# Working out the first scale vector on the tensor engine, beside the first shift vector

## The chip, the cores and the metric

The kernel runs on one core of a Trainium2 chip. The metric is the device time of one execution, in microseconds (us), as the median of several runs. The engines are named as in the profile: PE is the tensor engine (PEld its weight loads), DVE the vector engine, ACT the scalar engine, POOL is GpSimd, and SP is the engine whose queue issues most of the transfers.

## The reference, cut to what matters

The reference is a two-layer trunk over 256 context tokens and 256 latent tokens of width 1024. Each layer is a half-step SwiGLU feed-forward network, a token mixer, and a second feed-forward network. Before each of them the tokens are normalised, scaled and shifted by vectors that come from the conditioning c (latent tokens) or c_ctx (context tokens). Only the very first scale and shift matter here:

```
c_silu  = silu(c);  cc_silu = silu(c_ctx)
m  = c_silu  @ w_ada[0] + b_ada[0]        # 9 vectors of 1024; 0 is the first shift, 1 the first scale
mc = cc_silu @ w_ada[0] + b_ada[0]
h  = rms_norm(x, g_sub[0,0]) * (1 + m[1]) + m[0]      # and the same with mc for the context
gu = h @ ffn_w_in[0,0]                                # 1024 -> 2 x 2816
```

So shift and scale are two products of a vector with a 1024 x 1024 part of w_ada, each for two vectors (context and latent). They need 4 MB of weights each, and nothing of the first feed-forward network can begin without their first 128 entries.

## The kernel before, in words

Activations are kept transposed: a tile has 128 of the 1024 features in its partitions and the 512 tokens (256 context, 256 latent) in its columns, so the 1024 features are 8 tiles, k = 0 to 7. A product in fp32 accuracy is made from two parts of each operand, hi and lo: mm3 (L300) issues three matmuls, w.hi x.hi (L301), w.hi x.lo (L302) and w.lo x.hi (L303). A weight tile comes by DMA as raw fp32 (wr) and is split by a cast on ACT (L165) and a subtraction on DVE (L166) into wp.

The start of the program is start (L1508). After the sums of squares of the tokens and their inverse roots (ss, rr), it works through k = 0 to 7. For each k:

- load(k) (L1512) issues four transfers of 256 KB on SP: two halves of the scale's tile, from the transposed matrix w_adaT (tile 8 + k), and two halves of the shift's tile, from w_ada0.
- The shift's tile k goes to the tensor engine. pe_a(k) (L1525) is the first half of ada_tile (L388): 8 matmuls whose stationary operand is csp, the silu of both conditioning vectors padded to 32 columns, and whose moving operand is 128 columns of the tile; four groups of 32 partitions of the result collect two of them each. The profile shows each of these fp32 matmuls twice. ACT copies the result (adx, L396). pe_b(k) (L1530) is the second half: one matmul with the constant sel (L399) sums the four groups and turns the result into a column, and ACT adds the bias (L400) into M[0, 0].
- The scale's tile k is dotted with both vectors, row by row. dot(k) (L1536): for the context vector DVE multiplies and sums in one instruction per half (junk, L1542); for the latent vector POOL multiplies in place (L1544) and dot_sum(k) on ACT (L1549) sums. dot_end(k) (L1551) puts halves, gain and bias together with two small DVE instructions (L1554, L1555) into M[0, 1].
- Norm.h (L490), called by h_a(k) and h_b(k): DVE makes hn = x * scale * rr (L498), ACT adds the shift and rounds to hh (L503), DVE makes the rest hl (L505). Each of the three is issued once for the 256 context and once for the 256 latent tokens.
- first_whole (L551) then multiplies h(k) with the first four weight tiles: 4 x mm3 = 12 matmuls of 512 columns (gu). These are called a step below; there are 8 steps.

The order is written out by hand (manual schedule), so each engine's queue follows the program text:

```
def before(k):  ...
    WS.step()        # one half weight tile split: ACT L165, DVE L166 (while any are left)
    h_a(k + 1); dot_sum(k + 2); dot(k + 3); h_b(k + 1); dot_end(k + 2); load(k + 4)
# 12 matmuls of step k
def after(k):
    pe_b(k + 2); pe_a(k + 3)
```

So on PE the order is step 0, pe_b(2), pe_a(3), step 1, pe_b(3), pe_a(4), and so on to pe_a(7) in front of step 5 and pe_b(7) in front of step 6. Tiles of the kind slot (among them ar, the halves of load) rotate over 44 buffers. After step 7 the feed-forward network goes on with the next pair of weight tiles; those are split (L165, L166) after the last h on ACT's and DVE's queues. Later scale, shift and gate vectors are dotted by DVE alone from w_adaT (ada_dot, L403), which the change does not touch; it keeps cb, the conditioning repeated over all partitions, in use.

Of the kernel before, what the change touches and what calls it, by code (L numbers as in the profile page):

```python
# [15 lines left out]
OP = mybir.AluOpType  # L16
# [78 lines left out]
def trunk(ctx, tc, io):  # L95
# [289 lines left out]
        nc.sync.dma_start(t, src)  # L385
        return t

    def ada_tile(q, t, m, raw):  # L388

        p = bank("ada")  # L390
        for k in range(KD):
            r = slice(32 * (k % 4), 32 * (k % 4) + 32)
            PE.matmul(p[r, 0:128], csp[:, k, :], raw[k // 4][:, k % 4 * 128:k % 4 * 128 + 128], start=(k < 4),
                      stop=(k >= 4), skip_group_check=True)
        x = small("adx", 128, 3)
        ACT.copy(x, p[:, 0:128])  # L396
        yield
        p = bank("ada")
        PE.matmul(p[:, 0:2], x, C["sel"], start=True, stop=True)  # L399
        ACT.activation(m[:, t], p[:, 0:2], AF.Identity, bias=C["b_ada"][:, q * 8 + t:q * 8 + t + 1])  # L400
        yield

    def ada_dot(t, m, raw, vs=V2):  # L403
# [1104 lines left out]
    def start(n0, first_part, norm, then):  # L1508
        M[0, 0], M[0, 1] = new_m(), new_m()
        raws = {}  # L1510

        def load(k):  # L1512
            if k < KD:
                raws[k] = [[slot("ar") for _ in range(2)] for _ in range(2)]
                for ts, src in zip(raws[k], (io["w_adaT"][0, 8 + k], io["w_ada0"][k])):
                    for a, t in enumerate(ts):
                        nc.sync.dma_start(t, src[:, a * 512:a * 512 + 512])

        g0, b0 = C["g_sub"][:, 0:8], C["b_ada"][:, 8:16]
        bg = small("bg", 8, 1)  # L1520
        DVE.scalar_tensor_tensor(bg, b0, 1.0, g0, OP.add, OP.mult)

        steps = {}

        def pe_a(k):  # L1525
            if k < KD:
                steps[k] = ada_tile(0, k, M[0, 0], raws[k][1])
                next(steps[k])

        def pe_b(k):  # L1530
            if k < KD:
                next(steps[k])

        acc = [M[0, 1], small("dacc", 16, 1).rearrange("p (k v) -> p k v", v=2)]

        def dot(k):  # L1536

            if k < KD:
                junk = adap.tile([128, 1024], BF16, name=nm("junk"), tag="junk", bufs=1)
                for a, raw in enumerate(raws[k][0]):  # L1540
                    cols = slice(a * 512, a * 512 + 512)
                    DVE.scalar_tensor_tensor(junk[:, cols], raw, 1.0, cb[:, 0, cols], OP.mult, OP.mult,  # L1542
                                             accum_out=acc[a][:, k, 0:1])
                    POOL.tensor_tensor(raw, raw, cb[:, 1, cols], OP.mult)  # L1544

        def dot_sum(k):
            if k < KD:
                for a, raw in enumerate(raws[k][0]):
                    ACT.activation(raw, raw, AF.Copy, accum_out=acc[a][:, k, 1:2])  # L1549

        def dot_end(k):  # L1551
            if k < KD:
                g = g0[:, k:k + 1]
                DVE.tensor_scalar(acc[1][:, k], acc[1][:, k], g, bg[:, k:k + 1], OP.mult, OP.add)  # L1554
                DVE.scalar_tensor_tensor(acc[0][:, k], acc[0][:, k], g, acc[1][:, k], OP.mult, OP.add)  # L1555

        load(0)
        rest = WS.load(4, True)
        load(1)
        load(2)  # L1560
        for raw, src in rest:
            nc.sync.dma_start(raw, src)
        load(3)
        for d in range(KD):
            for v in V2:
                n0.add(d, v)
        for v in V2:
            ACT.activation(cb[:, v], cb[:, v], AF.Silu)
        ss = [n0.ss(v) for v in V2]
        run(ss[0], 1)  # L1570
        run(ss[1], 1)
        pe_a(0)
        for _ in range(12):
            for g in ss:
                run(g, 1)
        for v in V2:
            n0.rr(v)
        pe_b(0)
        dot(0)
        WS.want(4, False)  # L1580
        WS.step(4)
        dot_sum(0)
        dot_end(0)
        dot(1)
        pe_a(1)
        hs = {}

        def h_a(k):
            if k < KD:
                hs[k] = [n0.h(k, v) for v in V2]  # L1590
                for g in hs[k]:
                    next(g)

        def h_b(k):
            if k < KD:
                for g in hs[k]:
                    next(g)

        def before(k):

            if k == 0:
                h_a(0)
                pe_b(1)
                h_b(0)
                pe_a(2)
                dot_sum(1)
                dot(2)
                dot_end(1)
            WS.step()
            h_a(k + 1)  # L1610
            dot_sum(k + 2)
            dot(k + 3)
            h_b(k + 1)
            dot_end(k + 2)
            load(k + 4)

        def after(k):
            pe_b(k + 2)
            pe_a(k + 3)

        n0.before, n0.after = before, after
        first_part.run(n0, norm, first_whole, then=then)

# [62 lines left out]
def layout(inp):  # L1686
    import numpy as np
    f = {k: np.asarray(v) for k, v in inp.items()}
    A = np.ascontiguousarray

    def col(v):
        v = v.reshape(v.shape[:-1] + (-1, 128))
        return np.moveaxis(v, -1, 0).reshape(128, -1)

    def rep(v):
        return np.broadcast_to(v.reshape(1, -1), (128, v.size))

    cc = np.stack([f["c_ctx"], f["c"][0]])
    parts = {
        "c": cc.reshape(2, 8, 128).transpose(2, 1, 0).reshape(128, 16),  # L1700
        "b_ada": col(f["b_ada"]), "g_sub": col(f["g_sub"]),
        "lru_cw": col(f["lru_conv_w"][0]), "lru_cb": col(f["lru_conv_b"][0]),
        "b_gate": col(f["lru_b_gate"][0]), "lam": col(f["lru_lambda"][0]),
        "dn_cw": col(f["dn_conv_w"][0]), "g_norm": col(f["dn_g_norm"][0]), "g_final": col(f["g_final"]),
        "a_log": rep(f["dn_a_log"][0]), "dt_bias": rep(f["dn_dt_bias"][0]),
        "sel": (np.arange(128)[:, None] % 32 == np.arange(2)[None, :]).astype(np.float32),
    }
    out = {"cst": A(np.concatenate([parts[k] for k in CST], axis=1)), "cb": A(cc)}
    tok = np.concatenate([f["ctx"][0], f["x"][0]], axis=0)
    out["x0"] = A(tok.reshape(2, 256, 4, 2, 128).transpose(0, 2, 4, 3, 1))  # L1710

    def pack(w, mt):
        K, Mm = w.shape
        return A(w.reshape(K // 128, 128, Mm // mt, mt).transpose(2, 1, 0, 3).reshape(Mm // mt, 128, -1))

    out["w_ada0"] = pack(f["w_ada"][0][:, :1024], 128)
    out["lru_in"] = pack(f["lru_w_in"][0], 128)
    out["lru_out"] = pack(f["lru_w_out"][0], 128)

    out["lru_gate"] = A(f["lru_w_gate"][0].reshape(2, 2, 4, 2, 128, 256).transpose(0, 2, 4, 1, 3, 5)  # L1720
                        .reshape(2, 4, 128, 1024))
    out["dn_in"] = pack(f["dn_w_in"][0][:, :4096], 128)
    out["dn_ab"] = pack(f["dn_w_in"][0][:, 4096:], 32)[0]
    out["dn_out"] = pack(f["dn_w_out"][0], 128)
    p = np.arange(128)
    same = (p[:, None] // 64) == (p[None, :] // 64)
    up = same & (p[:, None] <= p[None, :])
    low = same & (p[:, None] >= p[None, :])
    eye = np.eye(128, dtype=bool)
    flip = (p + 64) % 128  # L1730
    i = np.arange(64)
    m = {"U1": up, "L1": low, "U1s": up & ~eye, "L1s": low & ~eye, "U1f": up[:, flip], "L1f": low[:, flip],
         "CH0": p[:, None] < 64, "CH1": p[:, None] >= 64,
         "cap": np.concatenate([p[:, None] % 64 <= i[None, :], p[:, None] % 64 >= i[None, :]], axis=1)}
    m["blk"] = same
    m["eye"] = p[:, None] % 64 == i[None, :]
    m["sel32"] = p[:, None] % 32 == np.arange(32)[None, :]
    out["msk"] = A(np.concatenate([m[k].astype(np.float32) for k in MSK], axis=1))
    out["w_adaT"] = A(f["w_ada"].transpose(0, 2, 1).reshape(2, 72, 128, 1024))

    out["ffn_in"] = A(f["ffn_w_in"].reshape(2, 2, 8, 128, 2, NJ, 128).transpose(0, 1, 5, 4, 3, 2, 6)
                      .reshape(2, 2, NJ, 2, 128, 1024))
    wo = f["ffn_w_out"].reshape(2, 2, 2, HALF, 128, 8, 128).transpose(0, 1, 2, 5, 4, 3, 6)
    out["ffn_out0"] = A(wo[..., :8, :].reshape(2, 2, 2, 8, 128, 1024))
    out["ffn_out1"] = A(wo[..., 8:, :].reshape(2, 2, 2, 8, 128, 384))
    return out
# [22 lines left out]
```

## Time and profile before

| | us |
|---|---|
| median of 3 runs (lowest, highest) | 1840.24 (1838.59, 1842.27) |
| the profiled execution's own time | 1840.58 |
| its span in the profile | 1838.8 |
| start of step 0 on PE | 25.04 |
| start of the matmuls behind step 7 | 67.16 |

Durations come from the one profiled execution. A busy time adds up instructions; instructions of PE overlap, so the distance between two starts on PE is what a matmul costs there. "Idle before" is the time that an engine stood still ahead of an instruction, with what ended it. [...]

### The profile page before, as it was taken

Reading aid. Unit: us, or ns where it says so; the run is one execution under the profiler, and the core shown is the slowest. Engines: PE = TensorE matmul, PEld = TensorE weight load, DVE = VectorE, ACT = ScalarE, POOL = GpSimd, SP = SyncE. Lnnn points to the kernel's source line nnn. Section 1 sums busy time; section 2 is a strip of 40 time slices with the busy share of each in tenths; the row PEclk is TensorE's granted clock in tenths of the full one; section 3 lists DMA queues with packets and bytes.
Section 4 is the critical chain, followed back from the end, with each engine's and each line's share of the span. In section 5 each row is a group of like instructions: output and inputs, shape, how many; then the busy total and the mean of one; then the engine's idle time right before and its main releaser. Section 6 shows DMA issues by size and latency. Waiting matters only on the chain.

```text
span 1838.8 us, 28624 instructions
## 1 busy us (share of the span) xinstructions
PE 1767.9 (96%) x10806; PEld 1534.4 (83%) x10806; DVE 1311.3 (71%) x2694; ACT 807.0 (44%) x1661; POOL 105.6 (6%) x146
## 2 busy tenths in 40 slices
PE   4999999999899999999999999999999989889997
PEld 3788888888778888888898888888997988689997
DVE  7877866787878767766657655555689978776565
ACT  5532222246884433233334331332478434655454
POOL 4100000000000000000000000000006330100000
PEclk9999999999999999999999999999999989989999
DMA  9354645452133666466633675654335550025653
GB/s 348 113 185 158 220 160 171 160 200 89 46 115 126 215 214 223 178 228 207 215 113 126 218 247 198 218 199 136 105 99 166 171 175 1 1 104 188 202 184 116
DMA packets 98059, 300.59 MB, mean 163 GB/s; under 512 B 10881, under 2 KB 20353, under 8 KB 97793
## 3 DMA queue, kind: packets, MB, share of 16 engines
q1 hardware_dynamic: 92160, 277.79, 44.7%
q0 software_dynamic: 5760, 20.97, 3.7%
q8 instruction: 85, 1.39, 0.3%
q14 instruction: 54, 0.43, 0.1%
HBM read 276.70 MB, written 22.02 MB: 162 GB/s over the span
## 4 chain that ended last, share of the span: by engine, by line
PE 79%; DVE 10%; ACT 5%; issue 4%; DMA 2%; POOL 0%; SPq 0%; POOLq 0%; ACTq 0%; DVEq 0%
PE gu L302 14%; PE gu L301 14%; PE gu L303 14%; PE fo L303 4%; PE fo L302 4%; PE fo L301 4%; PE tl L301 4%; PE tl L302 4%; PE tl L303 4%; DVE u L791 2%; PE p L1386 1%; PE gu L546 1%; PE gu L542 1%; PE gu L543 1%; PE p L1417 1%
## 5 line engine op out<-in xcount | busy, mean ns | idle before, releaser
L165 ACT CAST wp<-wr 128x512 fp32r<-128x512 f32 (+1 forms) x689 | 382.7, 607 | 279.8 <-DMA wr<-in_ffn_out_dram 68.1
L166 DVE TENSOR_TENSOR wp<-wr,wp 128x512 fp32r<-128x512 f32 (+1 forms) x689 | 433.5, 676 | 98.9 <-ACT wp L165 95.3
L302 PE MATMUL gu<-hl,wp 128*128 128x512 f32 (+1 forms) x1312 | 477.0, 364 | 8.0 <-DVE hl L505 8.0
L301 PE MATMUL gu<-hh,wp 128*128 128x512 f32 (+1 forms) x1312 | 476.9, 363 | 0.9 <-ACT hh L503 0.8
L303 PE MATMUL gu<-hh,wp 128*128 128x512 f32 (+1 forms) x1312 | 476.2, 363 | 0.0
L407 DVE SCALAR_TENSOR_TENSOR junk<-ar,cb 128x1024 bf16<-128x1024 f32 x224 | 273.8, 1223 | 22.6 <-DMA ar<-in_w_adaT_dram 18.8
L302 PEld LDWEIGHTS gu<-hl,wp 128*128 128x128 f32 x1312 | 247.3, 189 | 49.0 <-DVE hl L505 10.3
L301 PEld LDWEIGHTS gu<-hh,wp 128*128 128x128 f32 x1312 | 247.4, 189 | 41.2 <-ACT hh L503 1.6
L303 PEld LDWEIGHTS gu<-hh,wp 128*128 128x128 f32 x1312 | 247.5, 189 | 38.8
L657 ACT ACTIVATE sg<-gu 128x512 f32<-128x512 f32 (+1 forms) x88 | 47.9, 544 | 362.0 <-PE gu L303 352.3
L659 DVE TENSOR_TENSOR hf<-sg,gu 128x512 f32<-128x512 f32 (+1 forms) x88 | 54.5, 620 | 177.2 <-PE gu L303 130.3
L301 PE MATMUL tl<-hidh,wp 128*128 128x256 f32 (+1 forms) x418 | 139.1, 333 | 0.0
L302 PE MATMUL tl<-hidl,wp 128*128 128x256 f32 (+1 forms) x418 | 138.6, 332 | 0.0
L303 PE MATMUL tl<-hidh,wp 128*128 128x256 f32 (+1 forms) x418 | 138.6, 332 | 0.0
L301 PE MATMUL fo<-hidh,wp 128*128 128x512 f32 (+1 forms) x352 | 127.0, 361 | 0.0
L303 PE MATMUL fo<-hidh,wp 128*128 128x512 f32 (+1 forms) x352 | 127.0, 361 | 0.0
L302 PE MATMUL fo<-hidl,wp 128*128 128x512 f32 (+1 forms) x352 | 127.0, 361 | 0.0
L301 PE MATMUL f<-H,wp 128*128 128x256 f32 x320 | 93.2, 291 | 0.0
L303 PE MATMUL f<-H,wp 128*128 128x256 f32 x320 | 91.4, 286 | 1.0 <-DVE wp L166 1.0
L302 PE MATMUL f<-H,wp 128*128 128x256 f32 x320 | 91.2, 285 | 0.0
L301 PEld LDWEIGHTS tl<-hidh,wp 128*128 128x128 f32 x418 | 79.0, 189 | 7.9
L302 PEld LDWEIGHTS tl<-hidl,wp 128*128 128x128 f32 x418 | 79.0, 189 | 7.8
(322 smaller groups left out, 2794.7 us busy)
## 6 DMA issues: line engine op xcount, KB each, us to landing
wr<-in_ffn_in_dram SPq DMA_DIRECT2D x172, 512.0 KB, 4.7
ar<-in_w_adaT_dram SPq DMA_DIRECT2D x128, 512.0 KB, 3.6
wr<-in_ffn_out_dram SPq DMA_DIRECT2D x64, 512.0 KB, 4.9
kp<-wp SPq DMA_DIRECT2D x80, 256.0 KB, 7.2
wp<-kp POOLq DMA_DIRECT2D x40, 512.0 KB, 5.0
wr<-in_dn_in_dram SPq DMA_DIRECT2D x32, 512.0 KB, 3.7
wr<-in_ffn_out_dram SPq DMA_DIRECT2D x64, 192.0 KB, 3.5
wr<-in_lru_in_dram SPq DMA_DIRECT2D x16, 512.0 KB, 3.9
```

Of the source, the lines that this page charges most:

```text
L165: ACT.copy(dst.hi, src)
L166: DVE.tensor_tensor(dst.lo, src, dst.hi.bitcast(F32), OP.subtract)
L301: PE.matmul(out, w.hi, x.hi, start=start, stop=False)
L302: PE.matmul(out, w.hi, x.lo, start=False, stop=False)
L303: PE.matmul(out, w.lo, x.hi, start=False, stop=stop)
L407: DVE.scalar_tensor_tensor(junk, raw, 1.0, cb[:, v], OP.mult, OP.mult, accum_out=m[:, t % 8, v:v + 1])
L542: PE.matmul(p[:, cols], w.hi, x.hi, start=(k == 0), stop=False)
L543: PE.matmul(p[:, cols], w.lo, x.hi, start=False, stop=False)
L546: PE.matmul(p[:, cols], w(k * 128).hi, x.lo, start=False, stop=(k == KD - 1))
L657: ACT.activation(sg[:, cols], P[0][:, cols], AF.Silu)
L659: DVE.tensor_tensor(hf[:, cols], sg[:, cols], P[1][:, cols], OP.mult)
L791: DVE.scalar_tensor_tensor(uv[:, :, a:b], pv[:, :, a + sh:b + sh], cw(j), uv[:, :, a:b], OP.mult, OP.add)
```

## The change

The shift's and the scale's vector are now both made by ada_tiles, for one k at a time. load(k) fetches tiles k and 8 + k of w_ada0, which now holds 2048 columns, in place of a tile of w_adaT and one of w_ada0: the same four transfers of 256 KB. pe_a(k) issues 16 matmuls in place of 8, the scale's 8 into columns 128 to 255 of the same bank, and ACT copies 256 columns in place of 128. pe_b(k) issues two matmuls with sel in place of one, and ACT two activations: the shift with its bias, and the scale with the gain as factor and (1 + bias) * gain as bias. dot, dot_sum and dot_end, and with them all work of POOL and the multiplications of DVE in the steps, are gone. The order of what is left is as it was.

```diff
--- before.py
+++ after.py
@@ -385,19 +385,24 @@
         nc.sync.dma_start(t, src)
         return t
 
-    def ada_tile(q, t, m, raw):
+    def ada_tiles(raws, outs):
+
 
         p = bank("ada")
-        for k in range(KD):
-            r = slice(32 * (k % 4), 32 * (k % 4) + 32)
-            PE.matmul(p[r, 0:128], csp[:, k, :], raw[k // 4][:, k % 4 * 128:k % 4 * 128 + 128], start=(k < 4),
-                      stop=(k >= 4), skip_group_check=True)
-        x = small("adx", 128, 3)
-        ACT.copy(x, p[:, 0:128])
+        n = len(raws)
+        for i, raw in enumerate(raws):
+            for k in range(KD):
+                r = slice(32 * (k % 4), 32 * (k % 4) + 32)
+                PE.matmul(p[r, i * 128:i * 128 + 128], csp[:, k, :], raw[k // 4][:, k % 4 * 128:k % 4 * 128 + 128],
+                          start=(k < 4), stop=(k >= 4), skip_group_check=True)
+        x = small("adx", 128 * n, 3)
+        ACT.copy(x, p[:, 0:128 * n])
         yield
         p = bank("ada")
-        PE.matmul(p[:, 0:2], x, C["sel"], start=True, stop=True)
-        ACT.activation(m[:, t], p[:, 0:2], AF.Identity, bias=C["b_ada"][:, q * 8 + t:q * 8 + t + 1])
+        for i, (out, scale, bias) in enumerate(outs):
+            PE.matmul(p[:, 2 * i:2 * i + 2], x[:, i * 128:i * 128 + 128], C["sel"], start=True, stop=True)
+        for i, (out, scale, bias) in enumerate(outs):
+            ACT.activation(out, p[:, 2 * i:2 * i + 2], AF.Identity, scale=scale, bias=bias)
         yield
 
     def ada_dot(t, m, raw, vs=V2):
@@ -1512,47 +1517,26 @@
         def load(k):
             if k < KD:
                 raws[k] = [[slot("ar") for _ in range(2)] for _ in range(2)]
-                for ts, src in zip(raws[k], (io["w_adaT"][0, 8 + k], io["w_ada0"][k])):
+                for ts, src in zip(raws[k], (io["w_ada0"][k], io["w_ada0"][8 + k])):
                     for a, t in enumerate(ts):
                         nc.sync.dma_start(t, src[:, a * 512:a * 512 + 512])
 
-        g0, b0 = C["g_sub"][:, 0:8], C["b_ada"][:, 8:16]
+        g0, b0, b1 = C["g_sub"][:, 0:8], C["b_ada"][:, 0:8], C["b_ada"][:, 8:16]
         bg = small("bg", 8, 1)
-        DVE.scalar_tensor_tensor(bg, b0, 1.0, g0, OP.add, OP.mult)
+        DVE.scalar_tensor_tensor(bg, b1, 1.0, g0, OP.add, OP.mult)
 
         steps = {}
 
         def pe_a(k):
             if k < KD:
-                steps[k] = ada_tile(0, k, M[0, 0], raws[k][1])
+
+                steps[k] = ada_tiles(raws[k], ((M[0, 0][:, k], 1.0, b0[:, k:k + 1]),
+                                               (M[0, 1][:, k], g0[:, k:k + 1], bg[:, k:k + 1])))
                 next(steps[k])
 
         def pe_b(k):
             if k < KD:
                 next(steps[k])
-
-        acc = [M[0, 1], small("dacc", 16, 1).rearrange("p (k v) -> p k v", v=2)]
-
-        def dot(k):
-
-            if k < KD:
-                junk = adap.tile([128, 1024], BF16, name=nm("junk"), tag="junk", bufs=1)
-                for a, raw in enumerate(raws[k][0]):
-                    cols = slice(a * 512, a * 512 + 512)
-                    DVE.scalar_tensor_tensor(junk[:, cols], raw, 1.0, cb[:, 0, cols], OP.mult, OP.mult,
-                                             accum_out=acc[a][:, k, 0:1])
-                    POOL.tensor_tensor(raw, raw, cb[:, 1, cols], OP.mult)
-
-        def dot_sum(k):
-            if k < KD:
-                for a, raw in enumerate(raws[k][0]):
-                    ACT.activation(raw, raw, AF.Copy, accum_out=acc[a][:, k, 1:2])
-
-        def dot_end(k):
-            if k < KD:
-                g = g0[:, k:k + 1]
-                DVE.tensor_scalar(acc[1][:, k], acc[1][:, k], g, bg[:, k:k + 1], OP.mult, OP.add)
-                DVE.scalar_tensor_tensor(acc[0][:, k], acc[0][:, k], g, acc[1][:, k], OP.mult, OP.add)
 
         load(0)
         rest = WS.load(4, True)
@@ -1576,12 +1560,8 @@
         for v in V2:
             n0.rr(v)
         pe_b(0)
-        dot(0)
         WS.want(4, False)
         WS.step(4)
-        dot_sum(0)
-        dot_end(0)
-        dot(1)
         pe_a(1)
         hs = {}
 
@@ -1603,15 +1583,9 @@
                 pe_b(1)
                 h_b(0)
                 pe_a(2)
-                dot_sum(1)
-                dot(2)
-                dot_end(1)
             WS.step()
             h_a(k + 1)
-            dot_sum(k + 2)
-            dot(k + 3)
             h_b(k + 1)
-            dot_end(k + 2)
             load(k + 4)
 
         def after(k):
@@ -1713,7 +1687,7 @@
         K, Mm = w.shape
         return A(w.reshape(K // 128, 128, Mm // mt, mt).transpose(2, 1, 0, 3).reshape(Mm // mt, 128, -1))
 
-    out["w_ada0"] = pack(f["w_ada"][0][:, :1024], 128)
+    out["w_ada0"] = pack(f["w_ada"][0][:, :2048], 128)
     out["lru_in"] = pack(f["lru_w_in"][0], 128)
     out["lru_out"] = pack(f["lru_w_out"][0], 128)
```

## Rows read from the trace of the kernel before

**Rows 1.** The page, part 1: busy time of each engine over the span

```profile
PE 1767.9 (96%) x10806; PEld 1534.4 (83%) x10806; DVE 1311.3 (71%) x2694; ACT 807.0 (44%) x1661; POOL 105.6 (6%) x146
```

**Rows 2.** Windows, a stretch each: length, busy us (instructions) by engine, PEclk, DMA share, GB/s

```profile
0.00:67.16 67.16, 40.77 (x252) 29.86 (x253) 55.74 (x134) 36.67 (x97) 25.78 (x24) 0.95 0.67 246
...
200.00:400.00 200.00, 200.00 (x925) 167.41 (x924) 150.49 (x266) 59.68 (x115) 0.00 (x0) 1.00 0.53 179
```

**Rows 3.** Chain that ended last, 25.04 to 67.16: shares by line, then pieces (start, us)

```profile
by line: DVE hl L505 31.3%; DVE junk L1542 14.5%; PE gu L302 11.4%; PE gu L303 10.2%; PE gu L301 9.9%; DVE hn L498 7.6%; DVE wp L166 5.4%; issue 4.6%; DVE dacc L1554 4.3%; PE ada L393 1.4%; PE ada L399 0.6%; DVE m L1555 0.3%
...
36.60 0.78 DVE hn L498 x2
37.38 1.23 DVE junk L1542 x4
38.61 2.83 DVE hl L505 x2
41.81 0.69 DVE wp L166
...
56.47 0.43 PE gu L303
...
57.16 0.23 PE gu L302
```

**Rows 4.** Waits of PE, 25.04 to 67.16: total us, times, longest

```profile
PE gu L302 <- DVE hl L505: 8.0, 5, 2.9
```

**Rows 5.** Timeline, DVE's hl beside POOL at work, and with POOL idle

```profile
43.97 3.07 POOL L1544 TENSOR_TENSOR ar<-ar,cb 128x512 f32<-128x512 f32 x2 [2.81 <-DVE junk L1542]
...
44.42 2.90 DVE L505 SCALAR_TENSOR_TENSOR hl<-hn,m,hh 128x256 fp32r<-128x256 f32 x2
...
60.27 0.88 DVE L505 SCALAR_TENSOR_TENSOR hl<-hn,m,hh 128x256 fp32r<-128x256 f32 x2 [0.24 <-ACT hh L503]
```

**Rows 6.** Windows, steps 3, 4 and 7 of eight adjoining ones, and the sum of eight

```profile
44.88:50.83 5.95, 3.96 (x35) 2.93 (x31) 5.92 (x12) 3.02 (x11) 3.13 (x3) 1.00 0.29 94
50.83:58.25 7.42, 5.50 (x35) 4.07 (x31) 7.35 (x12) 2.87 (x11) 5.03 (x4) 0.77 0.05 17
...
64.30:67.16 2.86, 2.86 (x13) 2.17 (x12) 2.80 (x7) 2.84 (x5) 0.00 (x0) 1.00 0.00 0
sum 42.12, PE 33.37 PEld 25.06 DVE 40.42 ACT 22.67 POOL 19.39; mean PE 4.17 PEld 3.13 DVE 5.05 ACT 2.83 POOL 2.42
```

**Rows 7.** Timeline of PE and PEld: first rise of the clock, pe_b, pe_a, later stalls

```profile
29.31 0.51 PE L302 MATMUL gu<-hl,wp 128*128 128x512 f32 x1
...
43.87 0.42 PEld L399 LDWEIGHTS ada<-cst,adx 128*128 128x128 f32 x2
...
44.31 0.38 PEld L393 LDWEIGHTS ada<-ar,csp 128*32 128x32 f32 x16
...
44.88 0.19 PEld L301 LDWEIGHTS gu<-hh,wp 128*128 128x128 f32 x1 [0.20 <-issue]
...
47.38 0.50 PE L302 MATMUL gu<-hl,wp 128*128 128x512 f32 x1 [1.99 <-DVE hl L505]
...
53.25 0.66 PE L302 MATMUL gu<-hl,wp 128*128 128x512 f32 x1 [1.92 <-DVE hl L505]
```

**Rows 8.** Transfers of ar: SP's issues of the shift's tiles 3 and 7; time to landing

```profile
23.61 0.95 SPq L1517 DMA_DIRECT2D ar<-in_w_ada_dram  x2
...
34.34 0.96 SPq L1517 DMA_DIRECT2D ar<-in_w_ada_dram  x2
...
DMA to landing us min/median/max: 4.9/5.2/7.2
```

**Rows 9.** ACT's bias activation (min/median/max ns), and the weight splits behind step 7

```profile
L400 ACT ACTIVATE m<-ada,cst x8: 238/243/263, 17.5 to 61.8; 128x2 f32<-128x2 f32 x8
...
63.87 2.17 ACT L165 CAST wp<-wr 128x512 fp32r<-128x512 f32 x4
...
64.50 2.50 DVE L166 TENSOR_TENSOR wp<-wr,wp 128x512 fp32r<-128x512 f32 x4
```

## Prediction

> **What bounds the kernel now.** I read the page's busy times first: PE is busy for 96% of the span and no other engine comes near it [rows 1]. A change that takes work from DVE, ACT and POOL and gives some to PE can therefore only pay where PE stands still. The windows say where that is: in the first 67.16 us PE is busy for 40.77 us, while DVE is busy for 55.74; from 200 to 400 us PE is busy in every microsecond [rows 2]. The change lies inside that first stretch.
>
> Next comes the chain that ended last, cut to the eight steps (25.04 to 67.16 us). The reader should see that DVE, not PE, carries it: hl alone has 31.3% of it, junk (the scale's dots) 14.5% [rows 3]. The pieces of one step follow each other without a hole: two hn, 0.78 us, two junk with their sums, 1.23, two hl, 2.83, a wait and one weight split, 0.69; then the next hn 5.9 us after the last. Steps 1 to 4 all have this pattern. PE's waits agree: 8.0 us in five waits for hl [rows 4]. The reason for the long hl is in the timeline: two of them take 2.90 us while POOL works on its two multiplications (3.07 us), and 0.88 us once POOL is idle [rows 5]. So the scale's dots cost DVE twice, once by their own time and once by what POOL's share does to hl.
>
> The windows of the steps give the yardstick. All eight take 42.12 us, of which PE is busy for 33.37; steps 3 and 4 take 5.95 and 7.42 us, and step 7, in which PE waits for nothing, 2.86 [rows 6].
>
> **The change, part by part.**
>
> Removed per k: two junk with sums on DVE, the two small DVE instructions, two POOL multiplications and two ACT sums. What DVE keeps in a step is a split, two hn and two hl, 0.69 + 0.87 + 0.88 = 2.4 us with POOL idle [rows 3, 5], where a step now lasts 5.9. DVE then has time to spare, and the next thing to be late is PE itself.
>
> Added on PE: one more pe_a and one more pe_b for each k. In the step that runs at the full clock, the loads of pe_b begin at 43.87 (in the shadow of the last matmul, which ends its turn at 44.10), those of pe_a at 44.31, and the next step's load at 44.88 after 0.20 of idleness [rows 7]. So pe_b costs 0.21 and pe_a 0.57, of which 0.38 is its 16 loads and 0.20 the gap behind them. For the doubled pe_b I take 0.40 (bounds 0.21 and 0.42). For the doubled pe_a I take 0.57 + 0.38 = 0.95, the gap being paid once; the bounds are 0.57 and 1.14.
>
> The gap is a row's; why it is there, the row does not say ("issue"). [...]
>
> The stretch after the change, from the start of step 0 on:
> - Its start stays at 25.04. It stands behind pe_a(2), whose last quarter waits for the last half of load(2), and these transfers keep size, order and number. What the doubled pe_a(0) and pe_b(0) add on PE before that lies in waits for data. I cost it at nothing; if that cover were missing it would be one pe_a, 0.6.
> - Step 0 runs at the lower clock at first: matmuls stand 0.43 us apart there and 0.23 later [rows 3], and the first rise came at 29.3 [rows 7]. Without the wait for hl in it, ten matmuls at 0.43 and two at 0.23 make 4.86 us (bounds 2.86 and 12 x 0.43 = 5.16).
> - Seven steps without waits: 7 x 2.86 = 20.02.
> - pe_b(2) to pe_b(7): 6 x 0.40 = 2.40. pe_a(3) to pe_a(7): 5 x 0.95 = 4.75.
>
> The sum is 32.03 us against 42.12, so step 7 ends at 57.07 instead of 67.16: **10.1 us less**.
>
> Edits that I cost at nothing, and what covers them. ACT loses two sums per k and gains one activation of 0.24 us [rows 9] and 128 more columns to copy; a step of 4.2 us holds its cast, two hh, two activations and the copy (about 2.4). The chain from pe_a(k+2) to h(k+1) is copy, cast, split, hn, hh, hl: about 0.5 + 0.62 + 0.69 + 0.87 + 0.45 + 0.45 = 3.6 us with hn and hh overlapped by halves [rows 3, 5, 9], and hl is wanted 2.86 + 0.40 + 0.95 + 0.2 = 4.4 us after pe_a(k+2); if the cover fails, each step grows by the difference. SP's queue keeps its order. The tiles of w_ada0 have the size of those of w_adaT, and their buffers come free at pe_a(k), no later than before. The data arrive in time: the later pair of load(3) is issued from 23.61 to 24.56 and lands 5.2 us after that, at 29.8, while pe_a(3) ends at 31.2; that of load(7), issued by 35.3, lands at 40.5 [rows 8], when PE gets to pe_a(7) at 47. The weights behind step 7 are split in 2.17 and 2.50 us behind the last h [rows 9]; pe_b(7) ends two steps before the end, at 51.4, h(7) is done some 2.5 us later, and the first split stands at 55, ahead of 57.07.
>
> Behind step 7 PE is the bound [rows 2] and nothing is tied to a fixed time, so I let the whole gain reach the end. The profiled execution took 1840.58 us: 1840.58 - 10.1 = 1830.5. It stands 0.3 above the median, 1840.24, so the forecast is 1830.4.
>
> **The rivals.**
>
> *A new chain through ACT and DVE ends last* (chance 0.12). The 3.6 us above leave out the hand-overs between engines; with 0.2 for each of six it is 4.8, and if the two hl stay 0.6 us slower than with POOL idle, for another reason than POOL, it is 5.4. That is 1.0 more than the 4.4 at hand, in each of the four steps in which weights are split: 4 us of the gain go, and the time is 1834.4. For it: the chain is emitted across two iterations, behind the copy on ACT. Against: hl at 0.88 with POOL idle is in the trace, and one step of slack is written into the order.
>
> *The gain is hidden* (0.07): step 7 ends earlier but something behind it does not, the next weight tiles or their transfers. That gives 1840. Against: the weights' transfers wait for buffers that the splits free, and these splits move forward too; the DMA share in step 4 is 0.05 [rows 6], so there is room.
>
> *The clock stays low: slower than before* (0.05). [...] For it: in step 4 the granted clock is a mean of 0.77 [rows 6], after a wait that ended at 53.25 [rows 7]. Against: the wait of 1.99 us that ended at 47.38 [rows 7] left the clock at 1.00 throughout step 3 [rows 6], and in the sum above no such wait is left. [...]
>
> **How the numbers follow.** The forecast has 0.76. About 0.2%, 3.7 us, is what a measurement of this kernel can tell from no change. The forecast and the first rival lie beyond that: faster 0.88. Same is 0.07, slower 0.05. For the range, the bounds of the costs reach down to 10.1 + 2.0 (step 0) + 1.1 (pe_b) + 1.9 (pe_a) = 15.1 us of gain if all come together; I go to 13.4, 1827.0. Upward, 1.0 for pe_a, 0.6 for the start, 0.3 for step 0 and one fall of the clock (8 matmuls x 0.2 = 1.6) make 1834.0; half of the first rival's cases lie within another 1.5, so 1835.5.
>
> **What would show it right or wrong.** Right: hl at about 0.44 us each, no wait of PE for hl, steps of 2.86 with 1.3 to 1.4 us of pe_b and pe_a between them, POOL idle after the first 5 us, step 7 ending near 57, and the same distance from there to the end as before. Wrong: waits of PE for hh or hl that remain, waits for ar in pe_a(3) and later, matmuls 0.43 us apart beyond step 0, pe_a of more than 1.2 us, or a later wait that takes the gain back.

## The result, and the profile after

The changed kernel takes 1830.11 us, the median of 12 runs (1827.26 to 1839.76); the kernel before, timed beside it, 1841.41 (12 runs, 1838.59 to 1847.65). The ratio is 0.9942, with a 95% interval of 0.9927 to 0.9958: faster by 0.6%, 11 us. The prediction was 1830.4, with a range of 1827.0 to 1835.5.

The page's busy times, after; they answer to [rows 1]. POOL has lost 24.5 us and DVE 26, PE has gained 3:

```profile
span 1828.4 us, 28807 instructions
...
PE 1770.9 (97%) x10950; PEld 1538.7 (84%) x10950; DVE 1285.2 (70%) x2646; ACT 800.9 (44%) x1637; POOL 81.1 (4%) x130
```

The windows of the eight steps, after (length, busy us with instructions of PE, PEld, DVE, ACT, POOL, then PEclk, the mean granted clock as a share of full speed, then DMA share, GB/s); they answer to [rows 2, 6]:

```profile
24.38:29.67 5.29, 5.16 (x52) 4.01 (x48) 2.36 (x5) 2.31 (x6) 0.00 (x0) 1.00 1.05 402
29.67:33.97 4.30, 4.30 (x52) 3.59 (x48) 2.36 (x5) 2.31 (x6) 0.00 (x0) 1.00 1.05 405
...
38.29:42.61 4.32, 4.32 (x52) 3.59 (x48) 2.72 (x6) 2.31 (x6) 0.00 (x0) 1.00 1.03 420
42.61:46.93 4.32, 4.32 (x52) 3.59 (x48) 1.76 (x5) 1.69 (x5) 0.00 (x0) 1.00 0.37 148
46.93:50.17 3.24, 3.24 (x20) 2.72 (x17) 1.40 (x4) 1.18 (x3) 0.00 (x0) 1.00 0.03 5
50.17:53.02 2.85, 2.85 (x14) 2.34 (x14) 1.92 (x5) 2.12 (x6) 0.00 (x0) 1.00 0.00 0
53.02:55.74 2.72, 2.72 (x13) 2.25 (x12) 2.59 (x6) 2.69 (x5) 0.00 (x0) 1.00 0.02 3
```

Read the first and the second column against each other. PE is busy for the whole of every step but step 0, and steps 1 to 4, which have a pe_b and a pe_a behind them, last the same 4.3 us (step 0 has both too, but its matmuls start out further apart, 0.43 us). DVE, which was busy for nearly all of steps 3 and 4 before [rows 6], works 2.7 and 1.8 us of those. Step 7 ends at 55.74 us; before it was 67.16. So the front of the program is 11.42 us shorter, and the two spans differ by 1838.8 - 1828.4 = 10.4: what lies behind step 7 took 1771.6 us before and 1772.7 after, and the gain reached the end but for one microsecond. That microsecond can't be told from scatter: in the ten profiles of this case, all versions taken together, what lies behind step 7 took 1769.1 to 1778.2 us.

The chain that ended last, cut to the same stretch, has no line of DVE any more (compare [rows 3]):

```profile
by line: PE gu L301 24.1%; PE gu L303 20.7%; PE gu L302 20.3%; DMA ar<-in_w_ada_dram 20.1%; PE ada L396 14.3%; PE ada L403 5.4%; issue 0.1%
```

The DMA part is one piece of 6.29 us that begins ahead of the stretch, at 22.98: the last of the rows that pe_a(3) takes. They arrive at 29.27, when pe_a(3) is under way. The view of PE's waits, which had 8.0 us for hl [rows 4], has no row between 24.38 and 55.74; what is left of waiting stands with PE's weight loads, 0.40 us for these rows in pe_a(3), and then the gap behind every pe_a:

```profile
29.31 0.16 PEld L396 LDWEIGHTS ada<-ar,csp 128*32 128x32 f32 x8 [0.40 <-DMA ar<-in_w_ada_dram]
29.67 0.19 PEld L301 LDWEIGHTS gu<-hh,wp 128*128 128x128 f32 x1 [0.20 <-issue]
```

Why DVE is gone from the chain, its timeline shows: hl, in the changed kernel on L510, and in front of it split (L166) and hn (L503), in step 1; it answers to [rows 5]:

```profile
30.73 0.69 DVE L166 TENSOR_TENSOR wp<-wr,wp 128x512 fp32r<-128x512 f32 x1 [2.69 <-ACT wp L165]
31.34 0.87 DVE L503 SCALAR_TENSOR_TENSOR hn<-x,m,rr 128x256 f32<-128x256 f32 x2
...
32.45 0.88 DVE L510 SCALAR_TENSOR_TENSOR hl<-hn,m,hh 128x256 fp32r<-128x256 f32 x2 [0.24 <-ACT hh L508]
```

And PE between steps 1 and 2, with the doubled pe_b (L403) and pe_a (L396); it answers to [rows 7]:

```profile
32.53 0.50 PE L403 MATMUL ada<-cst,adx 128*128 128x2 f32 x4
32.96 1.08 PE L396 MATMUL ada<-ar,csp 128*32 128x128 f32 x32
33.97 0.50 PE L301 MATMUL gu<-hh,wp 128*128 128x512 f32 x1
```

From start to start pe_b takes 0.43 us and pe_a 1.01, of which 0.81 are its 32 loads and 0.20 the gap behind them. Before, the two took 0.21 and 0.57.

### The profile page after: what moved, and what is told of

Read it like the earlier page. It is cut to its first block, busy times and chain, and to the rows that moved or that the text cites. A ratio compares the mean times of both kernels' runs of the same rounds, so it can differ in the third digit from the quotient of the medians.

```text
span 1828.4 us, 28807 instructions
## 1 busy us (share of the span) xinstructions
PE 1770.9 (97%) x10950; PEld 1538.7 (84%) x10950; DVE 1285.2 (70%) x2646; ACT 800.9 (44%) x1637; POOL 81.1 (4%) x130
## 4 chain that ended last, share of the span: by engine, by line
PE 81%; DVE 8%; ACT 5%; issue 3%; DMA 2%; SPq 0%; POOL 0%; POOLq 0%; ACTq 0%; DVEq 0%
PE gu L301 14%; PE gu L302 14%; PE gu L303 14%; PE fo L303 4%; PE fo L302 4%; PE fo L301 4%; PE tl L301 4%; PE tl L303 4%; PE tl L302 4%; DVE u L796 1%; DMA wr<-in_ffn_in_dram 1%; PE p L1391 1%; PE gu L551 1%; PE gu L547 1%; PE gu L548 1%
## 5 line engine op out<-in xcount | busy, mean ns | idle before, releaser
L166 DVE TENSOR_TENSOR wp<-wr,wp 128x512 fp32r<-128x512 f32 (+1 forms) x689 | 432.5, 674 | 110.7 <-ACT wp L165 106.8
```

The source lines that it names most:

```text
L166: DVE.tensor_tensor(dst.lo, src, dst.hi.bitcast(F32), OP.subtract)
```

## The experiments

Two accounts fit what has been said so far. By the first, the step was set by DVE, and DVE was slow both because of its own dots and because POOL's multiplications made hl three times as long (2.90 us for two, 0.88 with POOL idle [rows 5]). By the second, DVE's own dots are enough. What the tensor engine's part costs, and what bounds the front now, are further questions. In each run below, "the steps" are the distance from the start of step 0 to the end of step 7: 42.12 us before, 31.36 after. The profiled executions differ in where step 0 starts, so this distance is what is compared. It scatters too: it was 31.36 and 31.83 in two profiles of the changed kernel. Three of the versions were run once, and the twelve runs of the changed kernel lie between 1827.26 and 1839.76 us; of a single run the distance tells more than the time.

**POOL's multiplications left out of the kernel before.**

```diff
-                    POOL.tensor_tensor(raw, raw, cb[:, 1, cols], OP.mult)
```

> Kernel before without POOL's multiplications (the latent half of the scale is then a sum of the raw rows); junk, sums and small instructions stay. Theory 1 (POOL at work makes hl three times as long, and that with junk set the step): hl falls from 1.45 to 0.44 us, the eleven slow ones give back about 11 us, step 7 ends near 56.5 in place of 67.16, and the time is near 1830, almost all of what the change brought. Rival A (the dots' own time on DVE set the step, hl is long for another reason): hl stays at 1.45, step 7 ends at 67, the time at 1840. Rival B (the gain came from falls of the tensor clock that are gone): something between, only if the waits of PE stay above 1 us and the 0.43 us spacing stays.

The steps took 30.37 us (23.76 to 54.13), the time was 1828.05 us (4 runs), the ratio to the kernel before 0.9928 (0.9907 to 0.9948). All sixteen hl are short, though every junk, sum and small instruction is still there. First the group of hl (durations min/median/max in ns), then steps 1 and 2 and all eight steps in the windows:

```profile
L505 DVE SCALAR_TENSOR_TENSOR hl<-hn,m,hh x16: 478/482/486, 23.3 to 50.9; 128x256 fp32r<-128x256 f32 x16
```

```profile
29.32:32.96 3.64, 3.64 (x34) 2.93 (x30) 3.13 (x11) 2.29 (x7) 0.00 (x0) 1.00 1.05 401
32.96:37.24 4.28, 3.92 (x34) 2.92 (x30) 4.02 (x14) 3.07 (x11) 0.00 (x0) 1.00 1.06 406
...
23.76:54.13 30.37, 29.49 (x188) 23.01 (x189) 27.77 (x78) 22.61 (x64) 0.00 (x0) 1.00 0.70 272
```

So the first account holds, and more sharply than I had it: taking POOL out of the way is enough for the whole gain. The dots that stay on DVE nearly fit beside PE; in step 2 PE still waits 0.36 us for hl, with DVE busy for 4.02 of 4.28 us. The long waits are gone: PE waited 0.9 us for hl in all.

Two things limit what this run shows. It does not do the latent half of the dots at all, so it gives the price of that half on POOL, and not what the work costs elsewhere. And a part of the gain is the tensor clock's, a share of what rival B says: before, the granted clock was a mean of 0.77 in step 4, which lasted 1.5 us longer than step 3 [rows 6], and here it is 1.00 over all eight steps. By an estimate from those two lengths that is some 1.5 of the 11.75 us. The kernel before has the long waits (up to 2.9 us [rows 4]) and the fall, this one neither; which part of the gain either would have alone was not tested.

**Both dots on DVE, in the kernel before.**

```diff
-                    POOL.tensor_tensor(raw, raw, cb[:, 1, cols], OP.mult)
+                    DVE.scalar_tensor_tensor(junk[:, cols], raw, 1.0, cb[:, 1, cols], OP.mult, OP.mult,
+                                             accum_out=acc[a][:, k, 1:2])
...
-                for a, raw in enumerate(raws[k][0]):
-                    ACT.activation(raw, raw, AF.Copy, accum_out=acc[a][:, k, 1:2])
+                pass
```

> Kernel before with both dots on DVE (two more junk a step in place of POOL's multiplications and ACT's sums). Theory 1: hl at 0.44, a second pair of junk at 1.23 us a step; the step is 5.9 - 1.95 + 1.23 to 1.45 = 5.2 to 5.4 us, step 7 ends near 63.5 and the time near 1837. Rival A: hl stays long and the step grows to about 7.1 us, step 7 ends near 74.5, time near 1848.

Step 7 ended at 63.78, the steps took 38.04 us, the one run 1836.58 us: 4 us of the 11 come from merely giving the work of POOL, and the sums of ACT behind it, to DVE, although DVE has two instructions with sums more a step. All sixteen hl are short here too (476 to 485 ns). Its window over the eight steps, with DVE busy for 36.17 of 38.04 us, says what is left to gain:

```profile
25.74:63.78 38.04, 33.75 (x188) 25.98 (x189) 36.17 (x104) 15.51 (x38) 0.00 (x0) 0.91 0.54 201
```

**POOL kept at work in the changed kernel.**

```diff
+        busy = adap.tile([128, 512], F32, name=nm("busy"), tag="busy", bufs=1)
+        POOL.memset(busy, 1.0)
+        for _ in range(24):
+            POOL.tensor_tensor(busy, busy, cb[:, 1, 0:512], OP.mult)
```

> The changed kernel with 24 multiplications of 128x512 on POOL on a buffer of its own, from about 14 to 51 us. Theory 1: hl at about 1.45 and the split at 0.9 us while POOL works, hn (one operand in PSUM) unchanged; DVE needs about 4.7 us a step against PE's 4.3, step 7 ends 1.5 to 3 us later than 55.74, time near 1832. Rival A: hl stays at 0.44, step 7 at 55.7, time 1830.

The direction was right, the size far off: 1841.47 us in one run, as long as the kernel before, with an engine at work whose result nobody reads. Step 0 started at 29.66 and the steps took 35.32 us. Read the lines of DVE beside POOL's block, which runs from 14.64 to 50.58:

```profile
14.64 35.94 POOL L1560 TENSOR_TENSOR busy<-busy,cb 128x512 f32<-128x512 f32 x24 [10.25 <-ACT cb L1552]
14.70 1.30 DVE L324 SCALAR_TENSOR_TENSOR ny<-rst,ny 128x2 f32<-128x2 f32 x2
...
21.52 6.70 DVE L166 TENSOR_TENSOR wp<-wr,wp 128x512 fp32r<-128x512 f32 x4 [2.83 <-ACT wp L165]
...
28.14 0.86 DVE L503 SCALAR_TENSOR_TENSOR hn<-x,m,rr 128x256 f32<-128x256 f32 x2
...
29.25 1.90 DVE L510 SCALAR_TENSOR_TENSOR hl<-hn,m,hh 128x256 fp32r<-128x256 f32 x2 [0.25 <-ACT hh L508]
...
50.46 0.88 DVE L510 SCALAR_TENSOR_TENSOR hl<-hn,m,hh 128x256 fp32r<-128x256 f32 x2 [0.24 <-ACT hh L508]
```

Four splits take 6.70 us, 1.68 each in place of 0.63. Two instructions of the inverse root on 2 columns take 1.30 together in place of 0.28. A pair of hl takes 1.90 and takes 0.88 again once POOL has ended. hn, whose second tensor (rr) lies in PSUM, stays at 0.86 for two throughout. Of these lines, those that stretch read two tensors in SBUF: a split, a pair of hl and the two of the inverse root each take about a microsecond longer, less than one POOL multiplication (1.38 us here, median), and however small they are themselves. How POOL holds them up, the lines do not show.

I had expected every hl at 1.45, as before [rows 5]. Here one of each pair is short and the other takes 1.50; before, the two took 2.90. And I had counted only hl and the splits of the steps: with the roots and the four splits ahead of it held up, step 0 began 5.3 us later, and the steps themselves took 4.0 more. Not all of the 4.0 is this stretching. Step 0 alone has 2.9 of it (6.41 us, where the profile of the changed kernel has 3.51): PE waits 0.74 us in it for hl, and its matmuls stay 0.43 us apart to its end. The other 2 us by which this run is longer lie behind step 7, where the profiles scatter by more than that.

**The scale's part of PE taken away from the changed kernel.**

```diff
+        for v in V2:
+            DVE.tensor_scalar(M[0, 1][:, :, v], g0, 1.0, None, OP.mult)
...
-                steps[k] = ada_tiles(raws[k], ((M[0, 0][:, k], 1.0, b0[:, k:k + 1]),
-                                               (M[0, 1][:, k], g0[:, k:k + 1], bg[:, k:k + 1])))
+                steps[k] = ada_tiles(raws[k][:1], ((M[0, 0][:, k], 1.0, b0[:, k:k + 1]),))
```

> The changed kernel without the scale's matmuls, copy and activation (the scale is the gain alone); its transfers stay. Theory 1 (PE is the bound from step 0 on): pe_a back from 1.01 to 0.57 us and pe_b from 0.43 to 0.21, step 7 ends 5 x 0.44 + 6 x 0.22 = 3.5 us earlier, near 52.2, time near 1826.5. Rival C (the rows' arrival or the chain through ACT and DVE is the bound by now): step 7 stays within 1 us of 55.7, with waits of PE for ar or hh in the place of the matmuls.

A step fell from 4.32 to 3.66 us, by exactly the 0.44 + 0.22 that pe_a and pe_b lost, with no wait of PE in its place:

```profile
22.36:50.95 28.59, 28.59 (x193) 23.01 (x190) 17.74 (x42) 15.72 (x37) 0.00 (x0) 1.00 0.83 315
27.74:31.40 3.66, 3.66 (x35) 2.93 (x31) 2.36 (x5) 1.95 (x5) 0.00 (x0) 1.00 1.05 401
```

PE is busy for all of the 28.59 us. So PE is the bound of these steps in the changed kernel, and the chain through ACT and DVE has at least 0.66 us a step to spare. For the rows the run settles only the shift's, since PE does not take the scale's here; in the changed kernel itself the scale's made one wait, the 0.40 us in pe_a(3).

The one run took 1827.18 us. The price of the scale on PE is 2.8 us by the steps (31.36 - 28.59), less than 3.5: that wait is gone as well, but step 0 lasted 4.59 us in place of 3.51, because its matmuls stood 0.43 us apart for longer in this execution. Step 0 also began 2.0 us earlier, at 22.36: pe_a(1) and pe_a(2) took 1.31 and 1.20 us ahead of it, and 2.55 and 1.93 in the changed kernel.

**What the changed kernel leaves on the table.** Three further versions were meant to beat both kernels. The first and the second ran with the changed kernel itself beside them.

> The changed kernel unaltered, beside the two below and the kernel before on the same chip: ratio to the kernel before 0.9942 again; step 0 starts at 24 to 25 us, step 7 ends 31.4 us later.

The ratio was 0.9941 (0.9914 to 0.9967) and the steps took 31.83 us (24.39 to 56.22), both as expected within the scatter.

The conditioning repeated over the partitions (cb) is not wanted any more until the steps are over, and its 1 MB lies ahead of all rows; in this version it comes late, and the first four weight splits move ahead of pe_b(0):

```diff
-    nc.sync.dma_start(cb, bass.AP(tensor=io["cb"].tensor, offset=io["cb"].offset, ap=[[0, 128], [1, 2048]])
-                      .rearrange("p (v k) -> p v k", v=2))
...
-        for v in V2:
-            ACT.activation(cb[:, v], cb[:, v], AF.Silu)
...
+        WS.want(4, False)
+        WS.step(4)
         pe_b(0)
-        WS.want(4, False)
-        WS.step(4)
...
+            if k in (5, 6):
+                ACT.activation(cb[:, k - 5], cb[:, k - 5], AF.Silu)
...
             load(k + 4)
+            if k == 3:
+                nc.sync.dma_start(cb, bass.AP(tensor=io["cb"].tensor, offset=io["cb"].offset,
+                                              ap=[[0, 128], [1, 2048]]).rearrange("p (v k) -> p v k", v=2))
```

> The changed kernel with the transfer of cb (1 MB, no longer wanted in the steps) behind load(7), its silu in steps 5 and 6, and the first four weight splits ahead of pe_b(0). Theory D (the start of step 0 is set by the arrival of load(2) behind 1 MB too much): step 0 starts 2.6 us (1.05 MB at 405 GB/s) earlier, near 21.9, the steps last 31.4 us as before, step 7 ends near 53.2, and the ratio to the kernel before is near 0.993. Rival E (the start is set by the tokens' sums and roots, by h(0) and the splits): step 0 starts at 24 as before, or waits of PE for hh or for ar in pe_a(3) take the gain back, ratio 0.994.

Step 0 started at 23.11, 1.3 us earlier than in the changed kernel, not 2.6. The steps took 31.88 us, without waits. The rest of the 2.6 us ran into the tokens' roots, as rival E has it for that half. The timeline of PE ahead of step 0 (lines have moved: L491 is rr, L401 pe_b, L394 pe_a):

```profile
16.20 1.11 PE L491 MATMUL rr<-ident,ny 128*128 128x128 f32 x4 [0.43 <-DVE ny L324]
17.11 0.85 PE L401 MATMUL ada<-cst,adx 128*128 128x2 f32 x4
17.89 1.93 PE L394 MATMUL ada<-ar,csp 128*32 128x128 f32 x32
20.31 1.01 PE L401 MATMUL ada<-cst,adx 128*128 128x2 f32 x4 [0.49 <-ACT adx L397]
21.25 1.93 PE L394 MATMUL ada<-ar,csp 128*32 128x128 f32 x32
23.11 0.80 PE L301 MATMUL gu<-hh,wp 128*128 128x512 f32 x1
```

No matmul waits for a transfer here; rr waits for the roots, and behind it come pe_b(0), pe_a(1), pe_b(1) and pe_a(2), the pe_a at 1.93 us where a later one takes 1.01. The time was 1831.18 (8 runs), the ratio 0.993 (0.9903 to 0.9957): no different from the changed kernel by this measurement.

The other two versions give DVE some rows of the scale again, without POOL: k = 3, 5 and 7, or 5 and 7 alone. For these k, load fetches the scale's tile from w_adaT again and pe_a takes the shift's tile alone (not shown).

```diff
+        DK = (3, 5, 7)
...
+        def dot(k, a):
...
+            for v in V2:
+                DVE.scalar_tensor_tensor(junk[:, cols], raw, 1.0, cb[:, v, cols], OP.mult, OP.mult,
+                                         accum_out=acc[a][:, k, v:v + 1])
...
+            for j in {0: ((3, 0), (3, 1)), 2: ((5, 0),), 3: ((5, 1),), 4: ((7, 0),), 5: ((7, 1),)}.get(k, ()):
+                dot(*j)
```

In the second of the two, DK is (5, 7) and the table is

```
{2: ((5, 0),), 3: ((5, 1),), 4: ((7, 0), (7, 1))}
```

> The changed kernel with the scale's rows k = 3, 5, 7 dotted by DVE (both vectors, no POOL) in the slack it now has. Theory 1 (PE's added pe_a and pe_b are the whole price of the new way, and DVE has about 1.9 us to spare a step): each of the three k gives back 0.44 + 0.22 us, together 2.0, so the steps last 29.4 us in place of 31.4, ratio near 0.993. Rival F (the longer DVE queue delays the split and hn of the next step): waits of PE for hh or hl appear and the steps last as long as before or longer.

> As e6_hybrid, but only rows k = 5 and 7 on DVE, row 5 half in step 2 and half in step 3, row 7 in step 4, each where its data have long landed. Theory 1 with rival F confined to row 3 (in e6 DVE stood waiting for the rows of k = 3 and then held hn back by 1.1 us): no wait of PE above 0.3 us, two k give back 0.44 + 0.22 us each, the steps last 1.3 us less than the changed kernel's 31.4 to 31.8, that is 30.1 to 30.5. Rival F in general (any dots on DVE delay hn by more than they save on PE): steps of 31.4 us or more with waits for hh.

Neither shortened the steps: 31.92 us (24.39 to 56.31) and 32.78 (24.82 to 57.60). The saving on PE is there (it is busy for 30.23 and 31.50 us of the steps, and for 31.83 in the second profile of the changed kernel), but waits take it back. The waits of PE in the steps, for the first and for the second of the two:

```profile
PE gu L301 <- ACT hh L508: 1.6, 2, 1.1
```

```profile
PE gu L301 <- ACT hh L508: 1.3, 1, 1.3
```

The longest wait of the first comes from row 3, where a dot stood at the head of DVE's queue for 0.76 us until its data came, and then the four dots of the row held up everything behind them until 32.22:

```profile
28.82 0.69 DVE L1551 SCALAR_TENSOR_TENSOR junk<-ar,cb 128x512 bf16<-128x512 f32 x1 [0.76 <-DMA ar<-in_w_adaT_dram]
...
32.22 0.69 DVE L166 TENSOR_TENSOR wp<-wr,wp 128x512 fp32r<-128x512 f32 x1
...
34.35 0.49 PE L301 MATMUL gu<-hh,wp 128*128 128x512 f32 x1 [1.08 <-ACT hh L508]
```

The second was meant to be rid of that, and it is; but it has a wait of the same size in front of step 6: the four dots of row 7 held DVE from 46.87 on, and hn for step 6 began behind them at 50.27. So in both the longest wait stands behind four dots in one step, 3.4 us of DVE. Step 0 was also longer in this execution (4.82 us). Row 5, with two dots in a step, brought no wait of PE in either version; the other wait of the first, 0.57 us in front of step 7, stands behind two dots of row 7. So rival F holds for rows 3 and 7 in the places tried, and not for row 5. The ratios, 0.992 (0.9891 to 0.9949) and 0.993 (0.9909 to 0.9952), are again no different from the changed kernel's. Row 5 alone on DVE, a spread of the dots over more steps, or rows whose step has a longer lead, was not tried. No version is shown to beat the change.

## Why the prediction was right

The forecast was 1830.4 us for 1830.11 measured. The mechanism held; that the number came within 0.3 us is in part luck, since errors of up to 1.4 us in its parts went against each other. The front of the program got 11.4 us shorter where 10.1 were forecast, and the part behind it took 1.0 longer. Step by step:

- *What bounds it.* "DVE, not PE, carries" the steps, and the scale's dots "cost DVE twice". The run without POOL's multiplications shows that the second of the two costs is enough for the whole gain: without it the steps take 11.8 us less than 42.12, and the dots' own time then fits almost wholly beside PE. That hl is long because of POOL was read from two lines that only stood side by side [rows 5]; the run with POOL kept busy shows it as cause (a pair takes 1.90 us beside POOL, and 0.88 once POOL has ended).
- *The next to be late is PE.* Shown, from step 1 on, by the full windows and by the run without the scale's matmuls.
- *The sum.* It was 32.03 us for the steps; 31.36 were measured. Its terms: each pe_b 0.40, measured 0.43; each pe_a 0.95, measured 1.01, with "the gap being paid once" as taken and the loads at 0.81 in place of 0.76; pe_a(3) took 0.4 us more, a wait for rows that the sum did not have (it had 1.4 us to spare there, but step 0 ended 2.0 us earlier than in the sum). The prediction names such a wait as a sign that it is wrong; in the second profile of the same kernel it is not there. The seven steps were 2.86 or a little less, as taken. Step 0 was 3.51 (24.38 to 27.89, the start of pe_b(2)) where I took 4.86 (ten matmuls at 0.43 and two at 0.23 make 4.76): the matmuls were 0.23 us apart from 25.8 on and not from 29.3. That term is no firmer than its bounds: in the second profile of the same kernel step 0 took 4.30. The range's 1.0 for pe_a, a gap paid twice, no run shows: behind each doubled pe_a of the changed kernel's steps stands one gap, 0.20 us.
- *The start of step 0*, which was to stay at 25.04, came at 24.38, 24.39 in the second profile. The prediction has it behind pe_a(2). For the kernel before this reading was wrong: there the first weight load of step 0 waited for hh, that is for h(0), which DVE's dots delayed. In the changed kernel hh is there earlier, and only the end of pe_a(2) is waited for. The same load before and after:

```profile
25.04 0.29 PEld L301 LDWEIGHTS gu<-hh,wp 128*128 128x128 f32 x1 [0.58 <-ACT hh L503]
```

```profile
24.38 0.29 PEld L301 LDWEIGHTS gu<-hh,wp 128*128 128x128 f32 x1 [0.38 <-issue]
```

  What the doubled work on PE ahead of step 0 costs, which the prediction put at nothing, was not nothing: without it step 0 began at 22.36, 2.0 us earlier (one run). That the start nevertheless moved by no more than 0.66 us, and forward, is luck: h(0) and the last rows of load(2) were both there earlier than before (pe_a(2) waited for rows up to 24.26 before, and not at all after), and the sum had neither. Why the rows came earlier is not settled.
- *What is hidden.* The weights behind step 7 were split in time: the next matmul after step 7 follows at 55.74 without a wait, and the gain reached the end to within the scatter of what follows, so the rival of a hidden gain fell. The rival of a clock that stays low fell too: from 25.8 on the matmuls stand 0.23 us apart. That PEclk is 1.00 in each of the eight windows would not settle it alone, since it is 1.00 over the first matmuls of step 0 as well.
- *The first rival*, a new chain through ACT and DVE, fell for the changed kernel: PE waited for neither hh nor hl. Waits of its kind, 1.3 to 1.6 us, appeared in the two versions that put dots back on DVE, but there the dots lengthen the chain, and not the hand-overs that the rival counts; those were not tested. By the run without the scale's matmuls the changed kernel is at least 0.66 us a step clear of it.

## What to carry to other kernels

When an instruction takes three times as long in one place as in another, look at what the other engines do in the same microsecond before counting it as that engine's work: here the silence of GpSimd alone brought as much as the whole change "to the tensor engine" (steps of 30.37 and of 31.36 us, from 42.12). The tensor engine was the cheap place for the work: the whole scale costs 2.8 us of the steps there, the latent half of it 7.7 on the vector engine (38.04 - 30.37), each read from one run. Work given to GpSimd to relieve the vector engine was not free here: beside it two hl took 2.90 us in place of 0.88 [rows 5]. And when the bound moves to another engine, price the new work there from start to start in a stretch without waits; the two such prices used here held to within 0.06 us each.

## What the hardware showed that was not expected

- Beside POOL's multiplications even very small instructions of DVE stretched: two of 2 columns, which read two tensors in SBUF, took 1.30 us beside POOL and 0.28 without. Step 0 began 5.3 us later behind such instructions, more than the 4.0 that the steps themselves lost.
- The matmuls of step 0 begin at about half the later rate (0.43 us from start to start, and 0.23 later), and the point at which this changes was another in two executions of the same program. In the two profiles of the changed kernel the starts are 0.43 us apart up to 25.40 in the first and up to 27.12 in the second, and 0.23 soon after. The texts here call this the lower clock, after the same two spacings in step 4 before [rows 3], where PEclk is a mean of 0.77 [rows 6]. But over these matmuls PEclk is 1.00 (the first window above): this stretch shows in the distances between the starts alone.

```profile
25.40 0.57 PE L303 MATMUL gu<-hh,wp 128*128 128x512 f32 x1
25.80 0.39 PE L301 MATMUL gu<-hh,wp 128*128 128x512 f32 x1
26.04 0.40 PE L302 MATMUL gu<-hl,wp 128*128 128x512 f32 x1
```

```profile
27.12 0.57 PE L301 MATMUL gu<-hh,wp 128*128 128x512 f32 x1
27.53 0.40 PE L302 MATMUL gu<-hl,wp 128*128 128x512 f32 x1
27.77 0.40 PE L303 MATMUL gu<-hh,wp 128*128 128x512 f32 x1
```
